# Strassen pairs of a float32 projection: three second products accumulate on a PSUM bank that has been read

## The chip, the cores and the metric

The kernel runs on one core of a Trainium2 chip. The metric is the device time of one execution in microseconds, and the time of a kernel is the median of its runs. TensorE (PE in the profile) multiplies matrices into PSUM, which has eight banks of 128 x 512 float32; VectorE (DVE), ScalarE (ACT) and GpSimd (POOL) do the rest, and SyncE (SP) issues most loads.

## The reference

Two decoder layers on 1024 tokens of 1024 channels. What matters here is the first step of a layer, one wide projection of the normalised tokens, whose output columns feed three branches:

```python
h = _rmsnorm(x, pre_g)
p = h @ w_in
(fq, fk, fv, ff, fg, dq, dk, dv, dg, cb, cc, cx, cg, mg) = _split_cols(p)
...
y_conv = cb * _short_conv(cc * cx, conv_w)
y_conv = y_conv * jax.nn.silu(cg)
gates = jax.nn.sigmoid(mg + b_m).reshape(b, s, N_BRANCH, D_MODEL)
m = (gates[:, :, 0] * (y_fox @ w_fox)
     + gates[:, :, 1] * (y_diff @ w_diff)
     + gates[:, :, 2] * (y_conv @ w_conv))
x = x + _rmsnorm(m @ w_o, post_g)
```

## The kernel before

Float32 matrices are multiplied as three passes over operands split into a high and a low part (`mm3`), so that one product of 512 input rows, 128 output columns and 512 tokens is 12 matmuls into one bank. The projection is computed transposed, 128 output columns (a chunk) at a time. For most chunks two of them are taken as a pair, and `strassen` forms their four blocks (chunk j = 0 or 1, token half h = 0 or 1) with seven products in place of eight. The products, in the order in which the kernel before issues them:

- P1 = b11·a11, P2 = b21·a12, P6 = t2·s2, P7 = t3·s3, P5 = t1·s1, P4 = t4·a22, P3 = b22·s4.
- Block (0,0) is P1 + P2, block (1,1) is P1 + P6 + P7 + P5, block (0,1) is P1 + P6 + P7 + P4 and block (1,0) is P1 + P6 + P5 + P3, with the signs inside the t and s operands.

The letters b and t are the weight operands, made anew for each pair by `emit_pair`: four differences on VectorE (L321), a cast to the high part on ScalarE (L318) and the low part on GpSimd (L319). They lie in four tiles: x holds b11 and b21, y holds t2 and t3, z holds t1 and t4, and b holds b22. The pool `ws` has three buffers of each kind, so a pair's fourth tile and all tiles of the next pair wait until a tile of a running pair is free. The letters a and s are token operands, made once a layer by `build_s` (L444 to L450) and kept.

There are 20 pairs a layer: six of the convolution branch (cb and cg of the chunks 0 and 1, then cc, cx, cb and cg of the chunks 2 and 3), two pairs of gates, four pairs of merge gates with the product of the convolution branch between them (`conv_merge`), and eight more pairs of gates, the last two with a SiLU. Every block goes to a function `use`: gates take a sigmoid and are written to DRAM, the convolution multiplies into its running blocks (`times`, on GpSimd at L546), and between the convolution's pairs VectorE runs the taps (L564, L567). Then come values, queries and keys, attention, merge and output projection, which the diff does not touch.

A scheduler puts the instructions of each engine in an order as the program is built; the order of the products on TensorE is mostly that of the code. `bank` deals the eight banks out in turn. TensorE's instructions wait on semaphores for their operands and for the last reader of a bank.

Of the kernel before, what the change touches and what calls it, by code (L numbers as in the profile page):

```python
# [34 lines left out]
# order of the query blocks (pairs) of a head, and of the FoX heads (pairs)  # L35
G_ORDER = (1, 2, 3, 0)
FOX_ORDER = (2, 3, 0, 1)
# work on the tensor engine that runs beside each attention pair or head
# [12 lines left out]
# weights of the attention's steps when work beside it is spread between them  # L51
W1F, W2F, W1D, W2D = 0.188, 1.324, 0.31, 1.574
# PSUM banks: logits, transposes, outputs, work beside the attention
# [3 lines left out]
def mm_us(n):  # L57
    """Time of a pass of n columns through the tensor engine."""
    return max(n, 128) * 0.000417


class Clock:
    """Estimated time of the tensor engine. What the other engines do after one of its steps is emitted
    when its turn would come, beside later steps, so that no engine's queue waits on an early entry."""
# [57 lines left out]
def interleave(main, main_cost, fill, fill_cost):  # L122
    """Emit the steps of main with those of fill spread evenly between them."""
    done, spent = 0.0, 0.0
    alive = True
    for w in main:
        done += w
        while alive and (spent < fill_cost * done / main_cost or done >= main_cost):
            try:
                spent += next(fill)  # L130
            except StopIteration:
                alive = False
    run(fill)


class Trunk:
# [35 lines left out]
    def transpose(self, out, x):  # L172
        """One block of 128 x 128, through the tensor engine."""
        self.nc.tensor.transpose(out, x, self.ident)  # L174
# [88 lines left out]
    def emit_load(self, key, kt, nco, eng):  # L263
        """DMA one weight tile [P, kt*nco] and split it into hi + lo float32r parts."""
# [18 lines left out]
    def load_w(self, key, kt, nco, eng="gpsimd"):  # L283
        """The next weight tile; the loads of the tiles after it are issued ahead of its use."""
# [19 lines left out]
    def emit_pair(self, l, i0, i1):  # L304
        """DMA two 128-column weight chunks, b1j and b2j their upper and lower halves, and form the split
        operands of a Strassen-Winograd step: b11, b21 | b12 - b11 (t1), b21 - t2 (t4) |
        b22 - t1 (t2), b22 - b12 (t3) | b22."""
# [38 lines left out]
    def mm3(self, ps, pairs, start=True, stop=True):  # L346
        """Accumulate the products of split operands: lo*hi + hi*lo + hi*hi for each k tile."""
        nc = self.nc
        n = len(pairs)
        for i, (wh, wl, xh, xl) in enumerate(pairs):  # L350
            nc.tensor.matmul(ps, wl, xh, start=start and i == 0, stop=False)  # L351
            nc.tensor.matmul(ps, wh, xl, start=False, stop=False)  # L352
            nc.tensor.matmul(ps, wh, xh, start=False, stop=stop and i == n - 1)  # L353

    def proj_g(self, w, h):
        """One 128-column chunk of the input projection, transposed, for token half h."""
# [18 lines left out]
    # ------------------------------------------------------------------ norm  # L375
    def rstd(self, ss, scale):
        """(ss * scale + EPS) ** -0.5 per partition."""
# [9 lines left out]
    def hk(self, h, k, o=0, n=512):  # L387
        """Tokens o..o+n of a half of hT, 128-row tile k: hi and lo."""
        return [t[:, k % 2, o:o + n] for t in self.hT[h][k // 2]]

    def norm_rows(self, xs, gB, hT, tb0, step):
        """rmsnorm of blocks of 128 tokens (rows of the tiles xs), transposed and split into hT."""
# [40 lines left out]
    # ------------------------------------------------------------------ Strassen-Winograd  # L433
    def build_s(self, L):
        """Sums of the quadrants of h (tokens x features), split: s1 = a21 + a22, s2 = s1 - a11,
        s3 = a11 - a21, s4 = a12 - s2. a21 itself waits in DRAM meanwhile."""
# [46 lines left out]
    def strassen(self, L, c0, c1, use, uv=None):  # L483
        """Two chunks of the input projection, transposed, with seven products in place of eight.
        use(j, h, x, ps, own): chunk j, token half h is x + ps; x may be overwritten if own."""
# [3 lines left out]
        def product(b, a):  # L489
            ps = self.bank()  # L490
            self.mm3(ps, [(w[b][0][:, k], w[b][1][:, k], *(t[:, k % 2] for t in L.a[a][k // 2])) for k in range(4)])
            return ps

        u, v = uv or (self.tmp(), self.tmp())
        nc.scalar.copy(u, product("b11", "a11"))
        use(0, 0, u, product("b21", "a12"), False)
        nc.vector.tensor_tensor(out=u, in0=u, in1=product("t2", "s2"), op=ALU.add)
        nc.vector.tensor_tensor(out=v, in0=u, in1=product("t3", "s3"), op=ALU.add)
        p5 = product("t1", "s1")
        nc.vector.tensor_tensor(out=u, in0=u, in1=p5, op=ALU.add)  # L500
        use(1, 1, v, p5, False)
        use(0, 1, v, product("t4", "a22"), True)
        use(1, 0, u, product("b22", "s4"), True)

    def plain(self, L, jobs):
        """Chunks of the input projection, transposed, [(chunk, use)]; the first token half of three
        comes before the second."""
# [8 lines left out]
    def total(self, x, ps, own):  # L516
        """x + ps in SBUF, or ps as it is."""
# [6 lines left out]
    # ------------------------------------------------------------------ conv  # L524
    def conv_pair(self, L, c, nplain):
        """Chunks c, c + 1 of the convolution branch; the first nplain projections without Strassen."""
# [52 lines left out]
    def conv_merge(self, L, dc):  # L579
        """Gates and convolution branch of chunks dc, dc + 1 of the merge, spilled."""  # L580
# [11 lines left out]
        def use(j, h, x, ps, own):  # L592
            sl = slice(h * 512, h * 512 + 512)
            y = self.total(x, ps, own)
            i = l * 24 + 16 + dc + j
            nc.scalar.activation(y, y, AF.Sigmoid, bias=self.par[:, i:i + 1])
# [7 lines left out]
    def gates_spilled(self, L, a, b):  # L604
        """Two chunks of gates, spilled for the merge."""
        nc, l = self.nc, L.l

        def use(j, h, x, ps, own):
            name, c = (a, b)[j]
            y = self.total(x, ps, own)  # L610
            if name == "mg":
                nc.scalar.activation(y, y, AF.Sigmoid, bias=self.par[:, l * 24 + c:l * 24 + c + 1])
            else:
                sg = self.tmp()
                nc.scalar.activation(sg, y, AF.Sigmoid)
                nc.vector.tensor_tensor(out=y, in0=sg, in1=y, op=ALU.mult)
# [4 lines left out]
    # ------------------------------------------------------------------ values  # L621
    def v_unit(self, L, kind, u, bank):
        """Values of four FoX heads or two differential heads (256 columns), tokens on partitions."""
# [6 lines left out]
        # per pair (or head): two tiles of four token blocks each  # L630
# [26 lines left out]
    def forget(self, L):  # L657
        """c = cumsum(log_sigmoid(ff + b)) for all heads, spilled as rows of a DRAM tile."""
# [9 lines left out]
        # log1p(e) = ln(u) * e / (u - 1) for u = fl(1 + e), and e where u == 1  # L668
# [23 lines left out]
    # ------------------------------------------------------------------ queries and keys  # L692
    def stack_evac(self, st, e, src, scale):
        """rows e*64.. of src -> hi in the same rows of st, lo in the other 64 rows."""
# [7 lines left out]
    def qk_unit(self, L, kind, p):  # L702
        """Queries and keys of two FoX heads or one differential head, split and stacked."""
# [38 lines left out]
    def gate_raw(self, L, name, c):  # L742
        """One chunk of gates before their SiLU, spilled for the merge."""
# [13 lines left out]
    # ------------------------------------------------------------------ attention  # L757
# [3 lines left out]
    def swap(self, qs, g):  # L761
        """Halves of a 256-query piece of each of two stacks, exchanged."""
# [9 lines left out]
    def logits(self, q, qsw, k, i):  # L772
        """-logits of query block i against its keys, with the causal guard: [(PSUM tile, first key, keys)]."""
# [538 lines left out]
```

## Time and profile before

| | us |
|---|---|
| median of 3 runs | 2570.14 |
| lowest, highest | 2569.18, 2570.54 |
| span of the profiled execution | 2573.8 |
| TensorE busy in it | 2439.4 |
| VectorE busy in it | 1699.8 |
| ScalarE busy in it | 1109.0 |
| GpSimd busy in it | 838.9 |

The span is the time from the first to the last instruction that the profiler saw. It is 3.7 us, 0.14%, over the median of the runs that were timed; what lies around the span in that one execution is not shown. In a timeline, the first number of a row is when an instruction starts, the second how long it takes (of the last of its matmuls for PE, which overlap: the next starts 0.23 us later). A bracket gives the idle time before it and what ended it.

### The profile page before, as it was taken

How to read it: one execution, taken by the hardware profiler on the slowest of the kernel's cores; microseconds unless marked ns; L12 is line 12 of the kernel's file. 1: busy time of each engine (PE TensorE's matmuls, PEld its weight loads, DVE VectorE, ACT ScalarE, POOL GpSimd, SP SyncE). 2: the span in 40 equal slices, each digit the busy share in tenths (PEclk: the TensorE clock that was granted, in tenths of full speed). 3: DMA queues.
4: the chain of work that ended last, by engine and by line, in shares of the span. 5: the costliest groups of instructions: out<-in, count | busy, mean ns of one | idle time of the engine just before them, and what ended most of it. 6: DMA issues, size and time to landing. Idle time of an engine off the chain costs nothing. (4 is left out here: it accounts for less than half of the span.)

```text
span 2573.8 us, 35788 instructions
## 1 busy us (share of the span) xinstructions
PE 2439.4 (95%) x13104; PEld 2051.8 (80%) x13104; DVE 1699.8 (66%) x3017; ACT 1109.0 (43%) x2282; POOL 838.9 (33%) x605
## 2 busy tenths in 40 slices
PE   7899999999999999899997999999999999989998
PEld 6677888888978778778976778888888787877798
DVE  6976464447687777767578654344486878777664
ACT  4224333336554554543433232233365545555333
POOL 1566334421112222361025652344211122232600
PEclk9899999999999999999998999999999999999999
DMA  4012223332222222563521122233321222225534
GB/s 167 33 50 95 92 96 111 107 132 70 63 69 68 63 87 64 169 220 129 194 90 41 50 95 89 75 117 130 93 80 53 69 68 75 82 70 186 202 119 180
DMA packets 111808, 260.35 MB, mean 101 GB/s; under 512 B 15744, under 2 KB 40576, under 8 KB 111632
## 3 DMA queue, kind: packets, MB, share of 16 engines
q1 hardware_dynamic: 56304, 183.33, 20.7%
q10 hardware_dynamic: 55328, 74.73, 9.4%
q8 instruction: 104, 1.70, 0.3%
q14 instruction: 72, 0.59, 0.1%
HBM read 183.48 MB, written 55.64 MB: 93 GB/s over the span
## 5 line engine op out<-in xcount | busy, mean ns | idle before, releaser
L279 POOL TENSOR_TENSOR wlo<-wraw,whi 128x1024 fp32r<-128x1024 f32 (+2 forms) x93 | 198.5, 2135 | 628.1 <-ACT whi L276 442.3
L351 PE MATMUL F<-ht,wlo 128*128 128x512 f32 x792 | 331.1, 418 | 0.0
L353 PE MATMUL F<-ht,whi 128*128 128x512 f32 x792 | 318.5, 402 | 0.0
L352 PE MATMUL F<-ht,whi 128*128 128x512 f32 x792 | 317.0, 400 | 0.0
L319 POOL TENSOR_TENSOR wlo<-sw,whi 128x512 fp32r<-128x512 f32 x160 | 224.6, 1414 | 228.6 <-ACT whi L318 203.1
L319 POOL TENSOR_TENSOR wlo<-wraw,whi 128x1024 fp32r<-128x1024 f32 x80 | 159.3, 1992 | 188.1 <-ACT whi L318 187.9
L318 ACT CAST whi<-sw 128x512 fp32r<-128x512 f32 x160 | 96.1, 619 | 245.6 <-DVE sw L321 106.1
L353 PEld LDWEIGHTS F<-ht,whi 128*128 128x128 f32 x792 | 150.8, 190 | 30.6
L276 ACT CAST whi<-wraw 128x1024 fp32r<-128x1024 f32 (+2 forms) x126 | 118.0, 939 | 129.8 <-PE F L353 41.9
L822 DVE TENSOR_TENSOR pt<-T,pt 128x512 fp32r<-128x512 f32 (+1 forms) x240 | 147.4, 632 | 37.4 <-ACT pt L821 35.7
L351 PEld LDWEIGHTS F<-ht,wlo 128*128 128x128 f32 x792 | 152.3, 192 | 24.2
L352 PEld LDWEIGHTS F<-ht,whi 128*128 128x128 f32 x792 | 151.5, 191 | 24.5
L821 ACT CAST pt<-T 128x512 fp32r<-128x512 f32 (+1 forms) x240 | 125.1, 544 | 91.3 <-PE T L174 66.1
L783 PE MATMUL S<-qk,qk 128*128 128x512 f32 (+2 forms) x384 | 141.7, 369 | 23.0 <-ACT p L922 21.1
L174 PE MATMUL T<-ident,p 128*128 128x128 f32 x864 | 135.3, 277 | 11.5 <-DVE p L858 6.6
L922 ACT ACTIVATE p<-S,sm 128x512 f32<-128x512 f32 (+2 forms) x192 | 110.5, 582 | 70.2 <-DVE sm L918 35.4
L916 DVE TENSOR_REDUCE sm<-S 128x1 f32<-128x512 f32 (+2 forms) x192 | 104.5, 551 | 48.5 <-PE S L787 29.6
L784 PE MATMUL S<-qk,sw 128*128 128x512 f32 (+2 forms) x384 | 131.8, 348 | 0.0
L318 ACT CAST whi<-wraw 128x1024 fp32r<-128x1024 f32 x80 | 66.8, 834 | 146.0 <-PE S L353 43.7
L351 PE MATMUL F<-whi,ht 128*128 128x256 f32 (+1 forms) x416 | 121.9, 293 | 4.2 <-DVE vd L373 4.2
L854 ACT ACTIVATE p<-p,sm 128x384 f32<-128x384 f32 (+7 forms) x128 | 99.5, 777 | 54.9 <-DVE sm L847 41.5
L321 DVE TENSOR_TENSOR sw<-wraw,sw 128x512 f32<-128x512 f32 x80 | 69.1, 863 | 81.3 <-POOL wlo L319 80.7
(390 smaller groups left out, 7249.2 us busy)
## 6 DMA issues: line engine op xcount, KB each, us to landing
wraw<-wt SPq DMA_DIRECT2D x128, 512.0 KB
mg<-tmp ACTq DMA_DIRECT2D x64, 256.0 KB
sw<-qk ACTq DMA_DIRECT2D x256, 64.0 KB
g<-mg SPq DMA_DIRECT2D x32, 512.0 KB
wraw<-wo SPq DMA_DIRECT2D x32, 512.0 KB
x<-x SPq DMA_DIRECT2D x24, 512.0 KB
wraw<-wbr SPq DMA_DIRECT2D x48, 256.0 KB
m<-tmp ACTq DMA_DIRECT2D x32, 256.0 KB
```

Of the source, the lines that this page charges most:

```text
L174: self.nc.tensor.transpose(out, x, self.ident)
L276: nc.scalar.copy(hi, raw)
L279: getattr(nc, eng).tensor_tensor(out=lo, in0=raw, in1=hi.bitcast(F32), op=ALU.subtract)
L318: nc.scalar.copy(w[0][:, o], f)
L319: nc.gpsimd.tensor_tensor(out=w[1][:, o], in0=f, in1=w[0][:, o].bitcast(F32), op=ALU.subtract)
L351: nc.tensor.matmul(ps, wl, xh, start=start and i == 0, stop=False)
L352: nc.tensor.matmul(ps, wh, xl, start=False, stop=False)
L353: nc.tensor.matmul(ps, wh, xh, start=False, stop=stop and i == n - 1)
L783: nc.tensor.matmul(ps[:, :wp], q[:, i * P:(i + 1) * P], k[:, c0:c0 + wp], start=True, stop=False)
L784: nc.tensor.matmul(ps[:, :wp], qsw[:, (i % 2) * P:(i % 2) * P + P], k[:, c0:c0 + wp], start=False, stop=not last)
L821: self.clock.later(0.1, lambda: nc.scalar.copy(hi, T[:, n0:]))
L822: done = self.clock.later(0.6, lambda: nc.vector.tensor_tensor(out=lo, in0=T[:, n0:], in1=hi.bitcast(F32), op=ALU.subtract))
```

## The change

`strassen` issues P1, P6, P7, P5, P2, P4, P3. P2 is accumulated on the bank of P1, P4 on the bank of P7 and P3 on the bank of P5, each after another engine has read the first sum there: ScalarE has copied P1 to u, VectorE has formed v = u + P7, and v + P5. So block (0,0) stands finished in PSUM, and its user reads it there; block (0,1) is one addition of u and a bank, block (1,0) too. Additions on VectorE are five a pair in place of seven. In the three `times` pairs of a layer that use `(0,0)` its product moves from GpSimd to VectorE, since it reads PSUM, and in the cc pair it becomes a copy on ScalarE. A pair takes four banks from the cycle, not seven.

```diff
-    def mm3(self, ps, pairs, start=True, stop=True):
+    def mm3(self, ps, pairs, start=True, stop=True, more=False):
...
-            nc.tensor.matmul(ps, wl, xh, start=start and i == 0, stop=False)
-            nc.tensor.matmul(ps, wh, xl, start=False, stop=False)
-            nc.tensor.matmul(ps, wh, xh, start=False, stop=stop and i == n - 1)
+            nc.tensor.matmul(ps, wl, xh, start=start and i == 0, stop=False, skip_group_check=more)
+            nc.tensor.matmul(ps, wh, xl, start=False, stop=False, skip_group_check=more)
+            nc.tensor.matmul(ps, wh, xh, start=False, stop=stop and i == n - 1, skip_group_check=more)
...
-        def product(b, a):
-            ps = self.bank()
-            self.mm3(ps, [(w[b][0][:, k], w[b][1][:, k], *(t[:, k % 2] for t in L.a[a][k // 2])) for k in range(4)])
+        def product(b, a, ps=None):
+            more = ps is not None
+            ps = ps or self.bank()
+            self.mm3(ps, [(w[b][0][:, k], w[b][1][:, k], *(t[:, k % 2] for t in L.a[a][k // 2])) for k in range(4)],
+                     not more, True, True)
             return ps
 
         u, v = uv or (self.tmp(), self.tmp())
-        nc.scalar.copy(u, product("b11", "a11"))
-        use(0, 0, u, product("b21", "a12"), False)
-        nc.vector.tensor_tensor(out=u, in0=u, in1=product("t2", "s2"), op=ALU.add)
-        nc.vector.tensor_tensor(out=v, in0=u, in1=product("t3", "s3"), op=ALU.add)
+        add = lambda o, x, ps: nc.vector.tensor_tensor(out=o, in0=x, in1=ps, op=ALU.add)
+        p1 = product("b11", "a11")
+        nc.scalar.copy(u, p1)
+        p6 = product("t2", "s2")
+        add(u, u, p6)
+        p7 = product("t3", "s3")
+        add(v, u, p7)
         p5 = product("t1", "s1")
-        nc.vector.tensor_tensor(out=u, in0=u, in1=p5, op=ALU.add)
-        use(1, 1, v, p5, False)
-        use(0, 1, v, product("t4", "a22"), True)
-        use(1, 0, u, product("b22", "s4"), True)
+        use(0, 0, None, product("b21", "a12", p1), False)
+        use(1, 1, v, p5, True)
+        use(0, 1, u, product("t4", "a22", p7), False)
+        use(1, 0, u, product("b22", "s4", p5), True)
...
-            y = self.total(x, ps, own)
+            s = self.total(x, ps, own)
+            y = self.tmp() if x is None else s
...
-                nc.scalar.activation(y, y, AF.Sigmoid, bias=self.par[:, l * 24 + c:l * 24 + c + 1])
+                nc.scalar.activation(y, s, AF.Sigmoid, bias=self.par[:, l * 24 + c:l * 24 + c + 1])
             else:
                 sg = self.tmp()
-                nc.scalar.activation(sg, y, AF.Sigmoid)
-                nc.vector.tensor_tensor(out=y, in0=sg, in1=y, op=ALU.mult)
+                nc.scalar.activation(sg, s, AF.Sigmoid)
+                nc.vector.tensor_tensor(out=y, in0=sg, in1=s, op=ALU.mult)
```

The rest of the diff takes comments out. The order of instructions is looked at in two places. The first is TensorE in a pair of gates of the first layer, where P1 ends (weights x are `whi` and `wlo` of one number, the bank of P1 is S_504 before and T_502 after); the pair before:

```order
L352 MATMUL S_504_2878<-ht_5_110,whi_467_2707 128x512
L353 MATMUL S_504_2878<-ht_4_109,whi_467_2707 128x512
L351 MATMUL T_505_2892<-ht_6_111,wlo_468_2708 128x512
L352 MATMUL T_505_2892<-ht_7_112,whi_467_2707 128x512
L353 MATMUL T_505_2892<-ht_6_111,whi_467_2707 128x512
```

The same place with the change:

```order
L353 MATMUL T_502_3083<-ht_5_110,whi_468_2917 128x512
L354 MATMUL T_502_3083<-ht_4_109,whi_468_2917 128x512
L352 MATMUL F_503_3097<-s2_99_534,wlo_473_2926 128x512
L353 MATMUL F_503_3097<-s2_100_535,whi_472_2925 128x512
L354 MATMUL F_503_3097<-s2_99_534,whi_472_2925 128x512
```

And where P5 ends in that pair with the change:

```order
L353 MATMUL S_505_3125<-s1_113_570,whi_474_2929 128x512
L354 MATMUL S_505_3125<-s1_112_569,whi_474_2929 128x512
L352 MATMUL T_502_3083<-ht_6_111,wlo_469_2918 128x512
L353 MATMUL T_502_3083<-ht_7_112,whi_468_2917 128x512
L354 MATMUL T_502_3083<-ht_6_111,whi_468_2917 128x512
```

P6, which needs the tile y, follows P1 at once, and P2 stands behind P5, back on the bank of P1. The second place is VectorE in the first pair of the convolution of the first layer, after the last tap (cv are the running blocks, uv the pair's u and v, sw a difference of weights), before:

```order
L567 SCALAR_TENSOR_TENSOR cv_74_333<-u_72_331,par_97,cv_74_333 128x1022
L321 TENSOR_TENSOR sw_127_657<-wraw_122_648,sw_127_657 128x512
L521 TENSOR_TENSOR tmp_137_706<-uv_121_647,O_136_693 128x512
L497 TENSOR_TENSOR uv_121_647<-uv_121_647,F_138_709 128x512
L498 TENSOR_TENSOR uv_121_647<-uv_121_647,S_139_723 128x512
L321 TENSOR_TENSOR sw_132_668<-wraw_123_649 128x512
```

With the change:

```order
L573 SCALAR_TENSOR_TENSOR cv_74_333<-u_72_331,par_97,cv_74_333 128x1022
L498 TENSOR_TENSOR uv_121_647<-uv_121_647,O_136_693 128x512
L552 TENSOR_TENSOR cv_73_332<-cv_73_332,T_135_679 128x512
L498 TENSOR_TENSOR uv_121_647<-uv_121_647,F_137_707 128x512
L527 TENSOR_TENSOR uv_121_647<-uv_121_647,S_138_721 128x512
L527 TENSOR_TENSOR tmp_139_761<-uv_121_647,F_137_707 128x512
```

The addition that reads the bank of P7 (F_137) stays third behind the last tap, as P7's addition (S_139) was fourth before; with the change P4 is written to that bank after it.

## Rows read from the trace of the kernel before

**Rows 1.** The page: busy time of each engine.

```profile
span 2573.8 us, 35788 instructions
PE 2439.4 (95%) x13104; PEld 2051.8 (80%) x13104; DVE 1699.8 (66%) x3017; ACT 1109.0 (43%) x2282; POOL 838.9 (33%) x605
```

**Rows 2.** Busy time by stretch: convolution pairs, then late gate pairs, first layer.

```profile
core 0: us, PE busy (x) PEld busy (x) DVE busy (x) ACT busy (x) POOL busy (x), PEclk, DMA share, GB/s
70.00:226.00 156.00, 140.00 (x566) 111.37 (x565) 124.58 (x116) 46.25 (x67) 103.10 (x59) 0.94 0.13 46
376.00:515.00 139.00, 139.00 (x601) 112.81 (x600) 63.80 (x85) 56.30 (x83) 64.19 (x43) 1.00 0.32 107
```

**Rows 3.** TensorE's waits for low parts of weights: total us, times, longest.

```profile
PE O L351 <- POOL wlo L319: 8.6, 1, 8.6
PE F L351 <- POOL wlo L319: 5.4, 3, 3.4
PE S L351 <- POOL wlo L319: 5.1, 3, 3.4
PE T L351 <- POOL wlo L319: 4.0, 1, 4.0
```

**Rows 4.** Timeline of TensorE, a gate pair: first matmuls of P1, P6, P7.

```profile
434.36 0.40 PE L351 MATMUL O<-ht,wlo 128*128 128x512 f32 x1
...
439.90 0.40 PE L351 MATMUL S<-s,wlo 128*128 128x512 f32 x1
...
442.71 0.40 PE L351 MATMUL T<-s,wlo 128*128 128x512 f32 x1
```

**Rows 5.** The same pair's weights: timelines of ACT, POOL and DVE; DVE's additions grouped.

```profile
434.61 1.14 ACT L318 CAST whi<-sw 128x512 fp32r<-128x512 f32 x2 [1.40 <-PE T L353]
...
435.31 2.55 POOL L319 TENSOR_TENSOR wlo<-sw,whi 128x512 fp32r<-128x512 f32 x2 [1.56 <-ACT whi L318]
...
436.64 1.76 DVE L321 TENSOR_TENSOR sw<-wraw 128x512 f32<-128x512 f32 x1 [1.40 <-POOL wlo L319]
...
438.44 0.62 ACT L318 CAST whi<-sw 128x512 fp32r<-128x512 f32 x1 [2.06 <-DVE sw L321]
...
439.14 1.29 POOL L319 TENSOR_TENSOR wlo<-sw,whi 128x512 fp32r<-128x512 f32 x1 [1.28 <-ACT whi L318]
...
L521 DVE TENSOR_TENSOR tmp<-tmp,S 128x512 f32<-128x512 f32 x42 | 28.7, 684 | 23.1 <-PE S L353 22.0 <-ACT tmp L495 0.6
```

**Rows 6.** Timeline of TensorE, convolution: three products after a wait, and the next.

```profile
118.16 0.50 PE L351 MATMUL F<-s,wlo 128*128 128x512 f32 x1 [0.76 <-POOL wlo L319]
...
178.13 0.50 PE L351 MATMUL S<-s,wlo 128*128 128x512 f32 x1 [1.20 <-POOL wlo L319]
...
1500.67 0.79 PE L351 MATMUL S<-s,wlo 128*128 128x512 f32 x1 [3.44 <-POOL wlo L319]
...
1505.95 0.63 PE L351 MATMUL T<-s,wlo 128*128 128x512 f32 x1
```

**Rows 7.** Pairs cc and cg: P1's start on PE, t3's low part on POOL.

```profile
129.39 0.40 PE L351 MATMUL S<-ht,wlo 128*128 128x512 f32 x1
...
136.02 1.30 POOL L319 TENSOR_TENSOR wlo<-sw,whi 128x512 fp32r<-128x512 f32 x1 [2.48 <-ACT whi L318]
...
189.37 0.40 PE L351 MATMUL S<-ht,wlo 128*128 128x512 f32 x1
...
194.32 3.01 POOL L319 TENSOR_TENSOR wlo<-sw,whi 128x512 fp32r<-128x512 f32 x2
```

**Rows 8.** First convolution pair of both layers: taps on DVE, P4 and P7 on PE.

```profile
102.42 8.03 DVE L567 SCALAR_TENSOR_TENSOR cv<-u,par,cv 128x1023 f32<-128x1023 f32 x4
...
102.70 0.63 PE L351 MATMUL F<-ht,wlo 128*128 128x512 f32 x1
...
1368.54 0.79 PE L351 MATMUL O<-s,wlo 128*128 128x512 f32 x1 [8.61 <-POOL wlo L319]
...
1374.56 7.00 DVE L567 SCALAR_TENSOR_TENSOR cv<-u,par,cv 128x1023 f32<-128x1023 f32 x4
```

More of the change, by code (lines that the diff above doesn't have):

```diff
@@ L593, in use @@
             sl = slice(h * 512, h * 512 + 512)
-            y = self.total(x, ps, own)
+            s = self.total(x, ps, own)
+            y = self.tmp() if x is None else s
             i = l * 24 + 16 + dc + j
-            nc.scalar.activation(y, y, AF.Sigmoid, bias=self.par[:, i:i + 1])
+            nc.scalar.activation(y, s, AF.Sigmoid, bias=self.par[:, i:i + 1])
             z = self.bank()
@@ L609, in use @@
             name, c = (a, b)[j]
-            y = self.total(x, ps, own)
+            s = self.total(x, ps, own)
+            y = self.tmp() if x is None else s
             if name == "mg":
-                nc.scalar.activation(y, y, AF.Sigmoid, bias=self.par[:, l * 24 + c:l * 24 + c + 1])
+                nc.scalar.activation(y, s, AF.Sigmoid, bias=self.par[:, l * 24 + c:l * 24 + c + 1])
             else:
                 sg = self.tmp()
-                nc.scalar.activation(sg, y, AF.Sigmoid)
-                nc.vector.tensor_tensor(out=y, in0=sg, in1=y, op=ALU.mult)
+                nc.scalar.activation(sg, s, AF.Sigmoid)
+                nc.vector.tensor_tensor(out=y, in0=sg, in1=s, op=ALU.mult)
             nc.scalar.dma_start(L.g[name][c, :, h * 512:h * 512 + 512], y)
```

## The prediction

> **What bounds the kernel now.** I read the engines' busy times first: TensorE is busy 95% of the span [rows 1]. A share of a whole span can hide stages, so I then read the pairs by stretch. In the late gate pairs TensorE is busy 139.00 of 139.00 us and VectorE only 63.80; in the convolution pairs TensorE is busy 140.00 of 156.00 and VectorE 124.58 [rows 2]. So in the gates nothing that VectorE is spared can show, and in the convolution something may. Which wait ends last there is in the list of TensorE's waits: 8.6, 5.4, 5.1 and 4.0 us in four groups, all for the low part of a weight tile that GpSimd makes (L319), 23.1 us in all [rows 3]. Nobody waits for an addition that the change removes. So I took one gate pair from the timelines and asked how much time the weights have to spare, since the change also moves P2, and with it the moment when each weight tile is wanted.
>
> **The additions.** 40 pairs lose two additions each, of 0.684 us [rows 5]: 55 us of VectorE. Six products come to VectorE from GpSimd and two become copies. In the gates this lies wholly beside TensorE's 139.00 of 139.00 us and is worth 0.
>
> **P2 moves, and takes its cover along.** P1 starts at 434.36, P6 at 439.90 and P7 at 442.71 [rows 4]: two products are 5.54 us, three are 8.35, one is 2.8. P7 wants t3, and t3 comes last out of a chain that starts when the pair before ends, because the tile z of the new pair takes a buffer that P3 frees: ScalarE casts z from 434.61, GpSimd makes its low part from 435.31, VectorE then forms t3 (436.64, 1.76 us, in a swap buffer that GpSimd has to release), ScalarE casts it at 438.44, GpSimd makes its low part from 439.14 for 1.29 us [rows 5]. It is done at 440.43, 6.07 us after P1 began. Before, P7 starts 8.35 us after P1 and has 2.28 to spare. With the change P2 no longer stands between, P7 is due after 5.54, and the chain, whose links and releases the new order keeps, is 0.53 us late. A wait also costs a little at the restart: the first matmul takes 0.50 instead of 0.40 [rows 4, 6]. I take 0.65 a pair. It holds for each pair that follows one without products of the branch between: 10 in a layer (the cx pair, one gate pair, the first merge pair, seven late gate pairs), so 20 x 0.65 = **13.0 us**. From below the bound is 0, if t3 were formed in the 0.69 us of an addition (1.07 less, and the chain ends at 5.00); above, about 25, if the SiLU pairs, which have more on ScalarE in the chain, wait a product's half more. I stay with the row.
>
> What makes t3 slow there is seen in the same rows: 1.76 us for a subtraction while GpSimd runs two low parts in a row until 437.86, against 0.684 for an addition of which one operand is in PSUM. The Trainium skill, SBUF — State Buffer, section SBUF: two separate sides, says that VectorE with two inputs in SBUF and GpSimd share a port pair that one holds for its whole instruction. The trace agrees; by it, the additions that go (one input each) do not block GpSimd, and their going does not shorten the chain.
>
> **The convolution pairs that wait already.** There GpSimd and VectorE have other work in the same queues, and t3 is later. In the cc pair its low part ends at 137.32, 7.93 us after P1; in the cg pair of the second chunks at 197.33, 7.96 us after P1 [rows 7]. Both fit under 8.35 and miss 5.54 by 2.4. Some is given back: VectorE has fewer additions ahead of t3, and GpSimd one product less in its queue, 1.3 to 1.4 us. I take 1.6 and 1.1, with 0 and 2.4 as ends. The cb pair of the second chunks waits 1.20 already [rows 6], behind the taps, which stay ahead of t3 in VectorE's order; its wait grows by 2.8 to 4.0. A wait of 3.44 in this trace is followed by a product of 5.28 us (1500.67 to 1505.95) instead of 2.8 [rows 6], at the lower of the two clock levels, while one of 1.20 is not; so 2.5 come on top: 5.3, with 2.8 as the lower end. The first gate pair, which has that 3.44, pays the clock already; its wait grows by 2.8 less what the SiLU's additions give back; I take 1.6, ends 0 and 2.8. Sum 9.6 a layer, **19.2 us**, ends 5.6 and 25.8.
>
> **The first convolution pair.** It starts while VectorE still makes the sums of the tokens, and TensorE waits, in the second layer 8.61 us before P7 [rows 8]. P2 needs none of these sums. Before, it runs ahead of the wait; with the change it comes behind: 2.8 a layer, 5.6. Here a new wait is also paid: P4 is written to the bank of P7, so it waits until VectorE has formed v. VectorE's queue has the four taps first, until 110.45 in the first layer [rows 8], then three instructions of some 0.68: 112.5. Before, P4 began at 102.70 [rows 8], and P3 and the next pair's P1 followed; with the change P2 and ten matmuls of that P1 fill the time to 109.4, and TensorE stands for some 3, behind by 3.6 in all. Queued behind that P4 are P3 and the whole next pair, whose t3 starts its chain at P3's end; its P7 waited 0.76 [rows 6] and now some 2.5 more. In the second layer the taps end at 1381.56 [rows 8] and P4 waits some 4 us, but there the next pair's P7 waits 4.0 already [rows 3], and that is merely spent earlier: 0.5. Together 5.6 + 3.6 + 2.5 + 0.5 = **12.2 us**, ends 5.6 and 22.
>
> The banks read meanwhile cost nothing in the gates: v is formed within a microsecond of P7, and P5 and P2 lie between. The Trainium skill, PSUM — Partial Sum Buffer, section Summary: rules for kernel authors, speaks against the change: when PSUM is read while a matmul runs, the matmul should have another bank, and the bank be guarded by a semaphore. The rows agree where VectorE is late, and by the rule alone each return to a bank would be a wait.
>
> **Sum.** 13.0 + 19.2 + 12.2 = 44.4 us. The profiled execution's span of 2573.8 [rows 1] would become 2618; its time is not shown, and its span lies 3.7 over the median of the runs, 2570.14, so I put the sum on the median: **2614**.
>
> **Rivals.** (a) Only the moved product counts: the relief on GpSimd's and VectorE's queues cancels what the convolution pairs lose, and 13.0 + 5.6 remain: 2589. For it: 124.58 us of VectorE in 156 [rows 2], where each addition less moves t3 forward. (b) The change does what its additions say: the 23.1 us of waits [rows 3] halve, since GpSimd's queue no longer stands on a product that waits for an addition, and t3 in the gates takes 0.69: 2570 - 11.5, so 2558. It decides in the gates, at a chain of 5.54 us: below it no pair there waits. Against it: that subtraction starts 1.2 us before GpSimd's second low part ends, in an order that does not change. (c) Both effects cancel: 2570, within 0.2%. (d) The banks: in all 12 convolution pairs P4 or P3 waits past VectorE's queue long enough to lower the clock, 2.5 each, 30 more: 2644. For it stands VectorE's load [rows 2], against it that only the first pairs have the taps ahead of their first additions while P1 to P5 run.
>
> **How the numbers follow.** My forecast 0.65, (a) 0.15, (d) 0.10, (b) 0.05, (c) 0.05. About 0.2%, 5 us, is what a measurement of this kernel can tell from no change; slower by more has 0.90, the same 0.05, faster 0.05. The range goes from 2588, just under (a), to (d)'s 2644, which takes in the ends of the terms added up except the outermost, and leaves out (b), (c) and some of (a) and (d).
>
> **What would show it.** Right: in the late gate pairs TensorE shows an idle of about half a microsecond before P7 in each pair, ended by GpSimd's low part, and the pair's period goes from 19.5 to 20.1; the waits for L319 grow from 23.1 to 50 or more; in the first pair P4 is released by VectorE. Wrong: no wait in the late gates, which means that t3 came sooner; waits on ScalarE or VectorE in the gates, which means that banks, not weights, bind; or a convolution stage as long as before.

## The result, and the profile after

The changed kernel takes 2607.81 us (median of 4 runs, 2603.95 to 2612.04), the kernel before 2569.94 beside it: slower by 37.9 us, a ratio of 1.0146 with a 95% interval of 1.013 to 1.0162. The forecast was 2614, slower, with a range from 2588 to 2644.

The page of the changed kernel, span and engines:

```profile
span 2607.4 us, 35591 instructions
PE 2445.7 (94%) x13104; PEld 2048.5 (79%) x13104; DVE 1647.6 (63%) x2943; ACT 1104.0 (42%) x2282; POOL 822.9 (32%) x599
```

Beside [rows 1], VectorE is spared 52.2 us, and the span is 33.6 longer. TensorE's busy time hardly moves; what grew is its idle time. Busy time by stretch, for the two stretches of [rows 2]:

```profile
70.00:226.00 156.00, 130.10 (x508) 101.99 (x507) 99.93 (x92) 39.53 (x58) 84.07 (x50) 0.91 0.12 41
376.00:515.00 139.00, 137.06 (x587) 109.72 (x586) 56.43 (x79) 52.32 (x77) 56.49 (x38) 1.00 0.29 106
```

In the convolution TensorE is busy 130.10 of 156 us instead of 140.00, at a granted clock of 0.91 instead of 0.94; in the late gates 137.06 of 139 instead of all of it. What it waits for, from the list of its waits (total us, times, longest):

```profile
PE T L352 <- POOL wlo L319: 30.8, 17, 10.3
PE F L352 <- POOL wlo L319: 12.0, 7, 5.2
PE S L352 <- POOL wlo L319: 6.5, 8, 3.1
PE S L694 <- DVE tmp L685: 3.2, 2, 1.6
PE T L352 <- DVE uv L498: 1.9, 1, 1.9
```

The waits for low parts of weights (L319) are 49.3 us in 32 places, where [rows 3] has 23.1 in 8. Only one wait is for a bank that VectorE still reads (the last row). The row on L694 is a wait after the gates; in the kernel before it was longer:

```profile
PE S L686 <- DVE tmp L677: 5.8, 2, 2.9
```

One late gate pair of the changed kernel, the timeline of TensorE (first matmuls of P1, P6, P7), then t3 on VectorE and its low part on GpSimd:

```profile
436.58 0.40 PE L352 MATMUL T<-ht,wlo 128*128 128x512 f32 x1
...
439.35 0.40 PE L352 MATMUL O<-s,wlo 128*128 128x512 f32 x1
...
442.68 0.50 PE L352 MATMUL F<-s,wlo 128*128 128x512 f32 x1 [0.36 <-POOL wlo L319]
```

```profile
438.86 1.76 DVE L321 TENSOR_TENSOR sw<-wraw 128x512 f32<-128x512 f32 x1 [1.40 <-POOL wlo L319]
...
441.35 1.28 POOL L319 TENSOR_TENSOR wlo<-sw,whi 128x512 fp32r<-128x512 f32 x1 [1.28 <-ACT whi L318]
```

The low part is done at 442.63, 6.05 us after P1 began; in [rows 5] it was 6.07. The chain is the same, but P7 now wants it after 5.5 us.

Of the signs that the prediction named, the wait before P7 came in the late gates (0.35 to 0.50 us) and with it the longer period (20.16 us in place of 19.50). The waits for L319 reached 49.3 us, just under the 50 that were named. P4 is released by VectorE in the first pair of the second layer alone.

The time of each pair, taken in the timelines from the first matmul of its P1 to that of the next pair's P1, in us (here "order", "additions" and the two t3 columns are experiments told below; the first two pairs are taken together, because their products interleave):

| | before | changed | order alone | additions alone | changed, t3 first | gates only, t3 first |
|---|---|---|---|---|---|---|
| first two pairs, layer 0 | 56.49 | 67.02 | 60.09 | 55.46 | 61.54 | 54.12 |
| first two pairs, layer 1 | 57.82 | 56.35 | 60.48 | 55.89 | 58.34 | 54.10 |
| cc, layer 0 | 19.50 | 21.19 | 23.28 | 19.50 | 19.52 | 19.50 |
| cb of chunks 2, 3, layer 0 | 20.99 | 26.42 | 27.34 | 21.01 | 23.28 | 19.52 |
| cg of chunks 2, 3, layer 0 | 19.50 | 20.66 | 21.54 | 19.50 | 19.51 | 19.80 |
| first gate pair, layer 0 | 25.91 | 27.38 | 24.26 | 19.66 | 19.93 | 21.80 |
| a late gate pair | 19.50 | 20.16 | 20.14 | 19.50 | 19.52 | 19.52 |

### The profile page after: what moved, and what is told of

It is laid out like the page before. It is cut to its first block, busy times and chain, and to the rows that moved or that the text cites. A ratio compares the mean times of both kernels' runs of the same rounds, so it can differ in the third digit from the quotient of the medians.

```text
span 2607.4 us, 35591 instructions
## 1 busy us (share of the span) xinstructions
PE 2445.7 (94%) x13104; PEld 2048.5 (79%) x13104; DVE 1647.6 (63%) x2943; ACT 1104.0 (42%) x2282; POOL 822.9 (32%) x599
## 5 line engine op out<-in xcount | busy, mean ns | idle before, releaser
L352 PE MATMUL F<-ht,wlo 128*128 128x512 f32 x816 | 340.8, 418 | 0.0
L354 PE MATMUL F<-ht,whi 128*128 128x512 f32 x816 | 327.8, 402 | 0.0
L353 PE MATMUL F<-ht,whi 128*128 128x512 f32 x816 | 326.2, 400 | 0.0
L319 POOL TENSOR_TENSOR wlo<-sw,whi 128x512 fp32r<-128x512 f32 x160 | 223.8, 1410 | 166.0 <-ACT whi L318 136.0
L319 POOL TENSOR_TENSOR wlo<-wraw,whi 128x1024 fp32r<-128x1024 f32 x80 | 151.9, 1898 | 324.2 <-ACT whi L318 324.2
L354 PEld LDWEIGHTS F<-ht,whi 128*128 128x128 f32 x816 | 155.1, 190 | 31.5
L353 PEld LDWEIGHTS F<-ht,whi 128*128 128x128 f32 x816 | 155.8, 191 | 25.1
L174 PEld LDWEIGHTS T<-ident,p 128*128 128x128 f32 x864 | 100.6, 142 | 28.1 <-DVE p L866 14.1
```

Source lines behind the costliest of these rows:

```text
L319: nc.gpsimd.tensor_tensor(out=w[1][:, o], in0=f, in1=w[0][:, o].bitcast(F32), op=ALU.subtract)
L353: nc.tensor.matmul(ps, wh, xl, start=False, stop=False, skip_group_check=more)
```

## Experiments

Two theories stand against each other. W: the loss is one of weights, since in the new order P2 no longer covers the making of t3. B: the loss is one of banks, since three products return to a bank that is read. Beside them stands the question of what the saved additions are worth.

### The order alone

```diff
-        nc.scalar.copy(u, product("b11", "a11"))
-        use(0, 0, u, product("b21", "a12"), False)
-        nc.vector.tensor_tensor(out=u, in0=u, in1=product("t2", "s2"), op=ALU.add)
+        k = self.tmp()
+        nc.scalar.copy(k, product("b11", "a11"))
+        nc.vector.tensor_tensor(out=u, in0=k, in1=product("t2", "s2"), op=ALU.add)
...
         nc.vector.tensor_tensor(out=u, in0=u, in1=p5, op=ALU.add)
+        use(0, 0, k, product("b21", "a12"), True)
```

(against the kernel before)

> The order of the changed kernel (P1, P6, P7, P5, P2, P4, P3), with the banks and the seven additions of the kernel before: every product has a bank of its own, nothing accumulates on a bank that was read. Theory W (weights: P2 no longer covers the chain that makes t3, and the tile x comes free later): as slow as the changed kernel or a little slower, since the convolution keeps two additions more a pair; the late gate pairs show the wait of 0.36 to 0.50 us before P7 for GpSimd's low part in each pair, and the time is 2600 to 2620 us. Theory B (the loss comes from accumulating on banks that are read meanwhile): the time of the kernel before, 2565 to 2580 us.

Measured: 2624.12 us, ratio 1.0208 (1.0189 to 1.0228). With a bank for each product and seven additions the new order is slower than the change itself. The late gate pair takes 20.14 us, and the waits for low parts sum to 59.1 us in 34 places. So the order by itself makes the kernel this slow; banks are not needed for it. The time is 16 us over that of the change and 4 us over the upper end of what was expected: the additions are worth more than thought.

### The saved additions alone

```diff
-        use(0, 0, u, product("b21", "a12"), False)
+        use(0, 0, None, product("b21", "a12"), False)
...
-        nc.vector.tensor_tensor(out=u, in0=u, in1=p5, op=ALU.add)
```

(in the order and with the banks of the kernel before; the users of a block as in the changed kernel, so the moves of products between GpSimd, VectorE and ScalarE are in it and are not priced apart)

> The kernel before with its order and banks, and two additions a pair left out (block (0,0) is P2 alone, block (1,0) lacks P5): what the saved additions are worth by themselves, with the same moves of work between GpSimd, VectorE and ScalarE as in the change. Theory W: nothing in the gates, a few us in the convolution pairs where VectorE's queue stands ahead of t3: 2562 to 2570 us. The rival that the additions were worth having (waits of 23.1 us for the low parts halve): 2559 us or less.

Measured: 2550.69 us, ratio 0.9922 (0.9901 to 0.9942). This is the rival's result: 19 us gained, not the 0 to 8 of theory W. The table says where: nothing in a late gate pair (19.50 both), but 6.25 us in the first gate pair of the first layer, which takes 19.66 instead of 25.91, and 6.21 in that of the second. There GpSimd splits the finished convolution (`ycl`) just ahead of t3's low part, and that waits for VectorE's last products of the convolution. GpSimd in the kernel before, where that pair's P1 starts at 208.87:

```profile
216.23 2.86 POOL L373 TENSOR_TENSOR ycl<-cv,ych 128x1024 fp32r<-128x1024 f32 x1 [1.71 <-ACT ych L372]
219.05 1.71 POOL L319 TENSOR_TENSOR wlo<-sw,whi 128x512 fp32r<-128x512 f32 x1
```

And with five additions, P1 at 207.75:

```profile
211.58 2.85 POOL L374 TENSOR_TENSOR ycl<-cv,ych 128x1024 fp32r<-128x1024 f32 x1
214.39 1.74 POOL L319 TENSOR_TENSOR wlo<-sw,whi 128x512 fp32r<-128x512 f32 x1
```

t3 is ready 8.4 us after P1 instead of 11.9. The wait of 3.43 us and the product at the lower clock behind it are gone together.

### P2 third

```diff
         p6 = product("t2", "s2")
         add(u, u, p6)
+        use(0, 0, None, product("b21", "a12", p1), False)
         p7 = product("t3", "s3")
         add(v, u, p7)
         p5 = product("t1", "s1")
-        use(0, 0, None, product("b21", "a12", p1), False)
```

> The changed kernel with one step moved: P2 is issued third (P1, P6, P2, P7, P5, P4, P3), still on the bank of P1 after ScalarE has copied it; P4 and P3 accumulate as in the changed kernel, five additions a pair. P7 is due 8.35 us after P1 again. Theory W: the waits before P7 in the late gates are gone, a pair takes 19.5 us, the convolution pairs wait as in the kernel before, and the time is 2560 to 2580 us. Theory B: all three accumulations are still there, so 2600 us or more, with TensorE's waits on VectorE or ScalarE.

Measured: 2571.71 us, ratio 1.0002 (0.999 to 1.0014). As W expects: all three accumulations are there, P7 is due three products after P1 again, and no late gate pair waits for weights. But it does not keep the 19 us of the additions: the profiled span is 12.9 us over that of the additions alone. Most of this, 9.8 us, lies in the first two pairs of the layers, 62.71 and 58.46 us instead of 55.46 and 55.89. In the first layer the scheduler did not keep P2 third there: TensorE runs the second half of P7 (F) and only then P2 (T), as in the changed kernel.

```profile
95.26 0.50 PE L352 MATMUL F<-s,wlo 128*128 128x512 f32 x1 [2.83 <-ACT s L449]
...
98.82 0.63 PE L352 MATMUL T<-ht,wlo 128*128 128x512 f32 x1
```

In the later pairs P2 comes back to the bank of P1 one product later and meets its reader (timeline of TensorE, a convolution pair and a gate pair):

```profile
180.80 0.50 PE L352 MATMUL T<-ht,wlo 128*128 128x512 f32 x1 [1.77 <-ACT uv L500]
...
383.02 0.50 PE L352 MATMUL T<-ht,wlo 128*128 128x512 f32 x1 [0.19 <-ACT tmp L500]
```

Returning to a bank has a price, then, where the reader is late: 1.77 us in the cb pair of each layer, and in five of the gate pairs 0.19 to 0.44. With three waits of P4 for VectorE (0.64, 0.64 and 1.13 us) it is 7.8 us in ten places.

### t3 first

```diff
-        z = new()
-        put(z, u, t1)
-        t3 = self.sw()
-        sub(t3, fb[:, d], fb[:, u])
-        sub(t2, fa[:, d], t2)
-        put(y, d, t3)
+        t3 = fb[:, u]
+        sub(t3, fb[:, d], t3)
+        put(y, d, t3)
+        z = new()
+        put(z, u, t1)
+        sub(t2, fa[:, d], t2)
         put(z, d, t2)
```

In the changed kernel:

> The changed kernel with its order and banks; only the making of weights is in another order: t3 is formed in place of b12 in the loaded tile (no swap buffer to wait for) and is split ahead of the tile z instead of behind it, so that its chain no longer starts when P3 of the pair before ends. Theory W: the 0.36 to 0.50 us waits before P7 in the late gates go (about 13 us in 20 pairs), and those of the convolution pairs shrink, so 2575 to 2592 us. Theory B: 2605 us or more, since the banks are as in the changed kernel. A third way, that t1 and t4 become late in t3's place: waits before P5 instead, and a time near 2608 us.

Measured: 2565.59 us, ratio 0.9977 (0.9964 to 0.999), 42 us below the changed kernel. Nothing in the products, banks or additions differs from it. This bears out W, and more than it asked (2575 to 2592): t1 and t4 are not late in their turn, and of 32 waits for low parts one is left. (The longest, of 10.3 us, has become one of 8.3 for the token sums. The edit does two things, it forms t3 in place and splits it ahead of z, and they are not priced apart.) What remains now is, for the most part, what returning to a bank costs in the convolution:

```profile
PE T L352 <- DVE uv L498: 5.6, 2, 3.7
PE T L352 <- POOL wlo L319: 4.6, 1, 4.6
PE F L352 <- DVE uv L498: 2.0, 1, 2.0
PE T L352 <- DVE tmp L498: 0.2, 1, 0.2
PE F L352 <- DVE tmp L498: 0.2, 1, 0.2
```

P4 waits for the addition that reads P7's bank (L498), 7.6 us in three convolution pairs; in 28 gate and merge pairs there are 0.4 us. The wait for L319 that is left, 4.6 us, is that of the second pair's P1 in the first layer. In the kernel before, the same edit:

> The kernel before with one edit: t3 is formed in place of b12 in the loaded tile and split ahead of the tile z, products, banks and additions as before. Theory W (a late t3 is what TensorE waits for): the waits for GpSimd's low parts in the convolution pairs and the first gate pairs go (0.76, 1.20 and 3.43 us in the first layer, 0.51, 4.03, 1.20 and 3.44 in the second), and with the three long ones a product at the lower clock each (2.5 us); the wait of 8.61 becomes one for the token sums. Together about 21 us: 2545 to 2556 us. Rival: t3 ahead makes t1 and t4 late, and the same time is waited before P5 and P4: 2565 us or more.

Measured: 2559.32 us, ratio 0.9948 (0.9932 to 0.9964), some 13 us gained where 21 were expected. The cb pair comes down to 19.52, the waits for low parts from 23.1 to 5.9, but the first gate pair still waits 1.85 us behind the split of the convolution, and the second pair of the second layer 2.16. So with t3 early in both, the change still loses, by 6 to 7 us (2565.59 against 2559.32, and the two intervals only touch): the late t3 is the larger part of its 38 us, and not all of them.

### Only the gates changed

```diff
+        if uv:
+            nc.scalar.copy(u, product("b11", "a11"))
+            use(0, 0, u, product("b21", "a12"), False)
+            add(u, u, product("t2", "s2"))
+            add(v, u, product("t3", "s3"))
+            p5 = product("t1", "s1")
+            add(u, u, p5)
+            use(1, 1, v, p5, False)
+            use(0, 1, v, product("t4", "a22"), True)
+            use(1, 0, u, product("b22", "s4"), True)
+            return
         p1 = product("b11", "a11")
```

(uv is given by the convolution pairs alone)

> The changed kernel, but the convolution pairs keep the order, banks and additions of the kernel before; the weights are made in the order of both kernels. Theory W: the late gate pairs lose 0.65 us each as in the changed kernel, 9 pairs a layer, the first gate pair some 2 us, and 1 to 3 us come back where the gates end: 2577 to 2590 us. If the loss of the change were one of the convolution alone: 2565 to 2572 us.

Measured: 2593.83 us, ratio 1.0082 (1.0064 to 1.01): 21 us, just above the 7 to 20 that were expected. The first gate pair's part is larger than the 2 us taken, 28.34 us instead of 25.91:

```profile
219.92 0.80 PE L352 MATMUL T<-s,wlo 128*128 128x512 f32 x1 [6.18 <-POOL wlo L319]
```

Its wait of 3.43 us, whose twin in the second layer stands in [rows 6], grew by 2.75, one product: P7 is due one product earlier, and t3 comes when it came. So the gate and merge pairs alone, with the convolution as before, lose about half as much as the change. (In the changed kernel the first gate pair loses less, 1.47 us, as the table shows.) With t3 first as well:

> t3 first as in the run before it; the convolution pairs keep the order, banks and seven additions of the kernel before, and only the 28 gate and merge pairs take the changed order with the three accumulations and five additions. Theory W: with t3 out of the way the accumulations cost nothing in the gates, and VectorE is less behind where the gates end: the time of the kernel before with t3 first, or up to 5 us less: 2541 to 2553 us. Theory B (a bank that was read costs a wait each time): 0.3 us or more a pair, so 8 us or more above the kernel before with t3 first.

Measured: 2555.11 us (2554.38 to 2556.45), ratio 0.9933 (0.9917 to 0.9949). On the same chip the kernel before with t3 first had 2558.02 to 2559.96, so the changed form of the gates is worth 4 us once t3 is early, as theory W expects; the time itself lies over the 2541 to 2553 that were named, as that of the kernel before with t3 first lay over its own forecast. A late gate pair takes 19.52 us with it: no cost of the banks there. In the first gate pair of each layer there is one, since P4 waits for VectorE. Two rows from the list of waits of this version, and the row of the wait after the gates from that of the kernel before with t3 first:

```profile
PE T L352 <- DVE tmp L498: 3.3, 2, 1.6
PE S L705 <- DVE tmp L696: 3.2, 2, 1.6
```

```profile
PE S L686 <- DVE tmp L677: 6.1, 2, 3.2
```

Of the gain, 2.9 us are the wait after the gates. This version beats both kernels, by 53 and 17 us.

### The first convolution pair

```diff
+        first = c0 == ("cb", 0)
+        if first:
+            use(0, 0, u, product("b21", "a12"), False)
         p6 = product("t2", "s2")
...
-        use(0, 0, None, product("b21", "a12", p1), False)
+        if not first:
+            use(0, 0, None, product("b21", "a12", p1), False)
```

> The changed kernel, but in the first convolution pair of each layer (cb of the chunks 0 and 1) P2 is issued second again, on a bank of its own, and added to the copy of P1; P4 and P3 accumulate there as in the changed kernel. In the changed kernel that pair and the next take 67.02 us in the first layer and 56.35 in the second, against 56.49 and 57.82 before. Theory X (the tile x: its buffer comes free only after P2, and the next pair's P1 waits 4.58 us for it in the first layer): P2 runs while TensorE waits for the token sums, the 4.58 and the slow matmuls after it go, and the first layer's two pairs take 57 to 60 us; the second layer gains 0 to 3: 2593 to 2601 us. Theory P4 (as in the prediction: P4, back on the bank of P7, waits for VectorE behind the taps): P4 only comes earlier and waits as much longer, and no more than 2.8 us a layer is gained: 2602 us or more.

Measured: 2615.38 us, ratio 1.0178 (1.015 to 1.0206), 7.6 above the changed kernel, which the overlapping intervals do not settle. The gain that theory X expects does not come: the first two pairs take 67.66 us in the first layer (67.02 without the edit) and 60.52 in the second (56.35). In the second layer it is P4 that waits, where the changed kernel waited 1.86:

```profile
1409.75 0.79 PE L352 MATMUL S<-ht,wlo 128*128 128x512 f32 x1 [4.83 <-DVE uv L498]
```

The late P2 does not lose time there: it fills time in which P4 would stand for its bank. In the first layer the next pair's P1 waits 4.22 us for its weights as it waited 4.58 before the edit, now on a buffer that another product frees: the cast of that tile starts at 102.19, when P7 has ended. So the edit did not make the tile x early, and what that would be worth is not measured. Theory P4 gave the sign of neither; it only bounded the gain, and that bound holds.

### Seven additions in the new order

```diff
-        nc.scalar.copy(u, p1)
+        k = self.tmp()
+        nc.scalar.copy(k, p1)
         p6 = product("t2", "s2")
-        add(u, u, p6)
+        add(u, k, p6)
...
-        use(0, 0, None, product("b21", "a12", p1), False)
-        use(1, 1, v, p5, True)
-        use(0, 1, u, product("t4", "a22", p7), False)
+        add(u, u, p5)
+        use(0, 0, k, product("b21", "a12", p1), True)
+        use(1, 1, v, p5, False)
+        use(0, 1, v, product("t4", "a22", p7), True)
```

> The changed kernel's order, banks and accumulations, with the two additions a pair that it saves put back (P1 and P5 are added twice, so two blocks hold other values; the product of block (0,0) is on GpSimd again): it has the additions of the run with the order alone (2624 us), and differs from it only in that three products return to a bank that was read. Theory W (order costs, additions help, banks cost nothing): 2618 to 2630 us. Theory B (returning to a bank costs some time too, which the saved additions pay for in the changed kernel): above 2632 us. If what helps in the change is the smaller number of banks and not the additions: 2605 to 2612 us.

Measured: 2629.15 us, ratio 1.0227 (1.0205 to 1.0249). In the new order the two additions are worth 21 us. Against the order alone (2624.12, 1.0189 to 1.0228) the banks cost 5 us, which the overlapping intervals do not settle. The waits for low parts are as long in both (59.5 and 59.1 us). The pair times differ most in the first two pairs: 65.15 us instead of 60.09 in the first layer, where P4 comes late, and 57.94 instead of 60.48 in the second. Half of the 21 lies where the prediction did not look, in the last pair of the gates with its two SiLU and just behind it: from that pair's P1 to the matmul that the list of waits names L694 or L696 it is 51.8 us in the changed kernel, in both layers, and 56.8 and 58.2 with seven additions. P7 there, in the second layer, with seven additions:

```profile
1846.38 0.80 PE L352 MATMUL T<-s,wlo 128*128 128x512 f32 x1 [2.67 <-POOL wlo L319]
```

In the changed kernel that wait is 0.48 us.

## Why the prediction came out as it did

The forecast was an increase of 44.4 us; 37.9 were measured. Term by term, from the table and its second layer:

- **The late gates and their like (13.0).** Right, in mechanism and size. Ten pairs in each layer wait 0.35 to 0.50 us before P7 for GpSimd's low part, and a late pair takes 0.66 more. Eight of them sum to 5.38 us in the first layer and 4.96 in the second; with the cx pairs (0.69, 0.64) and the last pairs (0.8 each, up to the start of P3) this is 13.2. The edit that makes t3 early takes it all away.
- **The convolution pairs that wait already (19.2).** Right: cc 1.69 and 1.70 (1.6 forecast), cg 1.16 and 1.12 (1.1), the first gate pair 1.47 and 1.03 (1.6), cb 5.43 and 4.35 (5.3). Together 17.95. The first gate pair's size is in part luck: 2.8 for the order less 1.2 for the additions was the working, but with the order alone that pair gets shorter (24.26 and 25.60 us, where the kernel before has 25.91 and 25.97). Only where the convolution is as before does its wait grow by a whole product (2.75 us, 28.34 for the pair). In the first layer's cb pair the wait and the slow product are plain (P6, P7, P5):

```profile
182.75 0.40 PE L352 MATMUL O<-s,wlo 128*128 128x512 f32 x1
...
189.69 0.80 PE L352 MATMUL F<-s,wlo 128*128 128x512 f32 x1 [3.97 <-POOL wlo L319]
...
194.98 0.63 PE L352 MATMUL S<-s,wlo 128*128 128x512 f32 x1
```

- **The first convolution pair (12.2).** Here the step failed, in its parts more than in its sum: 10.53 in the first layer (8.9 forecast) and a gain of 1.47 in the second (a loss of 3.3 forecast). The forecast said that P2 "comes behind" the wait for the sums and costs 2.8 a layer. In the second layer it cost nothing, since P4 has to wait for P7's bank anyway and P2 fills that time; what was left of P4's wait was 1.86 us, not some 4, and the next pair's P7 then waited 0.84 with no slow product, where it had waited 4.03 with one: that this product would be spared was left out. In the first layer the size was nearly right, and one cause was not. P4 was to stand for its bank behind ten matmuls of the next P1. TensorE stood ahead of them instead, for the tile x (T is P2 and then that P1, F is P4):

```profile
98.97 0.63 PE L352 MATMUL T<-ht,wlo 128*128 128x512 f32 x1
...
106.96 0.79 PE L352 MATMUL T<-ht,wlo 128*128 128x512 f32 x1 [4.58 <-POOL wlo L319]
110.88 0.40 PE L352 MATMUL F<-ht,wlo 128*128 128x512 f32 x1
```

  ScalarE's cast of that tile starts at 102.42, when P2 has ended, and GpSimd's low part is done at 106.91. I had followed t3's buffer through the new order, and not x's. But the bank was late as well. The rows are of ScalarE, GpSimd and VectorE; the last is the addition that reads P7's bank (F), behind the taps:

```profile
102.42 1.04 ACT L318 CAST whi<-wraw 128x1024 fp32r<-128x1024 f32 x1 [2.54 <-PE T L354]
103.54 3.37 POOL L319 TENSOR_TENSOR wlo<-wraw,whi 128x1024 fp32r<-128x1024 f32 x1 [2.30 <-ACT whi L318]
99.97 8.02 DVE L573 SCALAR_TENSOR_TENSOR cv<-u,par,cv 128x1023 f32<-128x1023 f32 x4
109.11 0.67 DVE L498 TENSOR_TENSOR uv<-uv,F 128x512 f32<-128x512 f32 x1
```

  P7's bank is free at 109.78, and P4 starts at 110.88, so an early tile x would have let P4 start at most 1.1 us sooner. With the order alone, where P4 has a bank of its own, it starts at 99.71, ahead of the next P1, and the two pairs take 60.09 us instead of 67.02 (65.15 with the same seven additions): here returning to a bank does cost time, as the prediction said. The next pair's P7 then waits 3.13 us instead of 0.76 (some 2.5 more were forecast), and the product after it takes 4.45 us instead of 2.88, which was left out.
- **After the gates (nothing forecast).** The profiles differ there by 5.3 us in favour of the change, half of it the wait on L694 (3.2 us instead of 5.8); where the other half lies is not shown. That VectorE is spared something was priced only inside the pairs. With 1.3 us by which the first pair starts sooner, the terms are 13.2 + 18.0 + 9.1 - 5.3 - 1.3 = 33.7, against the 33.6 us by which the spans differ; the medians differ by more, since the profiled execution of the kernel before was 3.7 us above its median.

**The additions** are the step that was furthest off, though the sum hides it. The prediction let them give back 0.8, 1.3 and 1.2 us in the cc, cg and first gate pairs, 6.6 us in two layers, on top of an order that would have cost 51. Measured, the order alone costs 54 (49 to 59 by its interval), and in the change the additions, less what the banks cost, give back 16 of it; by themselves they are worth 19 in the old order and 21 in the new one with accumulations. So the order was sized nearly right and the additions at less than half, and that is the 6.5 us by which the forecast was too high. The sentence "In the gates this lies wholly beside TensorE's 139.00 of 139.00 us and is worth 0" is right for the late gates, where TensorE is busy all the time, and wrong for the last pair of the stage, over which the same argument was stretched. For the first gate pair, which had been given 1.2 us, it depends on the order: 6.25 us are gained there in the old one and none in the new one (25.54 us with seven additions, 27.38 in the changed kernel); why is not shown. Rival (b) had its part on the queues in some measure right: the additions alone beat its 2558, though the waits fell from 23.1 to 15.0 us and not by half.

Of the rivals, (a) falls with the 17.95 us of the convolution pairs that waited already, (b) and (c) with the waits in the late gates, and (d) with the list of waits, where one wait of the pairs is for a bank. The Trainium skill, PSUM — Partial Sum Buffer, section Summary: rules for kernel authors, asks that a matmul have another bank than the one being read while it runs. Returning to a bank has a price in these runs where the reader is late: P4 waits up to 4.83 us for VectorE's addition, P2 1.77 for ScalarE's copy. No row of the kernel before could show that, since there each product has a bank of its own. In the gates the same return costs 0.4 us in 28 pairs with t3 first, and 3.3 us, all in the two first gate pairs, where the gates alone are changed.

## What to carry to other kernels

When a change moves a step, list what that step covered: a product that stands ahead of a late operand is worth its whole length to that operand, and here 2.8 us of cover were moved to save two additions of 0.7 us. Ask of the operand why it is late before ordering the work around it; six lines that made t3 ahead of z turned a loss of 38 us into a gain of 4 (the kernel before gains some 13 from the same lines, and stays ahead by 6 to 7). And relief on an engine that is off the path is priced at the edges of a stage, where its queue runs late, not in the middle, where it shows nothing.

## What was not expected of the hardware

The lower clock after a wait does not cost a fixed sum. P7 after a wait of 3.97 us took 5.29 us in the first layer (189.69 to 194.98) and after the same wait in the second 4.44 (1481.95 to 1486.39); after 3.13 us it took 4.45 (122.98 to 127.43), after 1.42 us 2.89. An undisturbed product takes 2.78. TensorE's busy time and granted clock (the 0.50 and 0.62) in the first two of these products:

```profile
189.69:194.98 5.29, 5.29 (x12) 4.13 (x13) 4.68 (x6) 0.00 (x0) 0.00 (x0) 0.50 0.00 0
1481.95:1486.39 4.44, 4.44 (x13) 3.53 (x14) 4.44 (x6) 0.00 (x0) 0.00 (x0) 0.62 0.00 0
```

The first runs at 0.50 throughout, the lower of the two levels (1.2 of 2.4 GHz); in the second the clock is at the lower level for a part of the product only. What decides between them is not shown. The forecast's 2.5 us for each long wait is the upper of the sizes that were seen.
